# Expert input products of a decoder layer: three 256-column products a weight tile instead of one of 512 and one of 256 columns

## Chip, cores, metric

The kernel runs on one core of a Trainium2 chip. The metric is the device time of one execution in microseconds (us); the median of several runs is compared. TensorE is called PE in the profile (its weight loads PEld), VectorE DVE, ScalarE ACT, GpSimd POOL and SyncE SP.

## What is computed

The reference is one decoder layer on 256 tokens with 2048 channels, in f32: attention and a convolution side by side, then a channel mixer that picks 16 experts for each of 8 heads out of 16384. The change touches the first product of that mixer. Cut to it:

```python
a = jnp.einsum('td,ted->te', x_c, u_emb[e_c])      # x_c: normed tokens, u_emb: 16384 x 2048
coef = (jax.nn.gelu(a) * g_c).astype(v_emb.dtype)
return jnp.einsum('te,ted->td', coef, v_emb[e_c])
```

The kernel doesn't gather. It computes the product of all 16384 experts with all 256 tokens, applies gelu, multiplies by a matrix of gates that is zero where an expert wasn't picked, and multiplies the result by all rows of `peer_v`.

## The kernel before

**The stream.** All large weights go through one stream, whose order is a list made ahead. A piece is 128 x 512 of weights, so four weight tiles of 128 x 128. SP loads two pieces at a time into `raw` (4 buffers). ACT rounds a piece to a short float format, `hi` (L153, 5 buffers), and DVE subtracts it from the full value, `lo` (L159, 4 buffers). Products of PE are then made as hi times hi, hi times lo and lo times hi, which together are near f32. `Stream.piece` issues for piece number p, in this order: the cast `hi` of piece p + 4, the subtraction `lo` of piece p + 3, the matmuls of piece p, and then one step of each job that is under way. A job is a generator that issues a few instructions at each step (evacuations of PSUM, the choice of experts, the scatter of gates), so the place of every instruction in its engine's queue follows from the count of pieces.

**Projections.** `Stream.proj` makes one output tile of 128 x 256 from 16 weight tiles, so 4 pieces. For each weight tile it issues three matmuls of 256 columns into one sum: hi of the weight with hi of the input (L200), hi with lo (L201), lo with hi (L202). `Stream.proj2` makes the same sum in another order: for the four weight tiles of a piece first hi of the weight with 512 columns, which are hi and lo of the input side by side (L213), so that two partial sums lie side by side in a PSUM bank, and then for the four weight tiles lo of the weight with 256 columns of hi, into the second of these sums (L217). Each matmul has a weight load of its own, in both.

**The expert inputs.** 128 tiles `u_tile(i1)` of 4 pieces each, 512 pieces, from 1005.9 us to 1751.2 us of the profiled execution. The input `h2` holds hi and lo of each 128 channels side by side, and `h2hi`, `h2lo` are views of it. The last 8 query projections before it (L1184) use `proj` on these two views; in between stand the score matmuls of a head (L1077, 8 matmuls of 128 columns each). After each tile a job evacuates PSUM: a copy of the second sum to `ut` (ACT L1194 for the first 48 tiles, DVE L1196 for the other 80), an addition of the first sum (DVE L1198), gelu into `C` (ACT L1202), and for tokens whose gates are in `C` already, gelu into `ut` (L1204) and a product (DVE L1208). PSUM has two `acc` buffers.

**Beside it.** During the first 48 tiles DVE works on the choice of experts (`top_steps`), and PE does nothing else, but for the last 8 matmuls of L1077 at the start and three pairs of transposes at the end (L1139). During the other 80 tiles `g_steps` makes the matrix of gates, four tokens at a time: DVE and ACT build one-hot tiles (L1219, L1225), PE multiplies them (L1246, groups of 8 f16 matmuls), and DVE and ACT bring the result into `C` (L1234, L1236). There are 64 such groups, one every four to five pieces. Then follows the output product with `peer_v` (L1333 to L1335, matmuls of 512 columns).

Of the kernel before, what the change touches and what calls it, by code (L numbers as in the profile page):

```python
# [9 lines left out]
F32 = mybir.dt.float32  # L10
# [3 lines left out]
AF = mybir.ActivationFunctionType  # L14
# [5 lines left out]
T = 256  # L20
D = 2048
KT = 16
# [50 lines left out]
def build(nc, tc, d):  # L73
    ctx = ExitStack()
    ve, sc, pe, sp = nc.vector, nc.scalar, nc.tensor, nc.sync
# [53 lines left out]
    class Stream:  # L129
# [63 lines left out]
        def proj(self, bank, nk, xhi, xlo, evac):  # L193

            ps = bank()
            for k0 in range(0, nk, 4):
                def mm(hi, lo):
                    for j in range(4):
                        k, o = k0 + j, j * 128
                        pe.matmul(ps, hi[:, o:o + 128], xhi[:, k], start=(k == 0), stop=False)  # L200
                        pe.matmul(ps, hi[:, o:o + 128], xlo[:, k], start=False, stop=False)  # L201
                        pe.matmul(ps, lo[:, o:o + 128], xhi[:, k], start=False, stop=(k == nk - 1))  # L202
                self.piece(mm)
            return self.add(evac(ps))

        def proj2(self, bank, nk, x, evac):

            ps = bank()
            for k0 in range(0, nk, 4):
                def mm(hi, lo):  # L210
                    for j in range(4):
                        k, o = k0 + j, j * 128
                        pe.matmul(ps.rearrange("p a t -> p (a t)"), hi[:, o:o + 128],  # L213
                                  x[:, k].rearrange("p a t -> p (a t)"), start=(k == 0), stop=False)
                    for j in range(4):
                        k, o = k0 + j, j * 128
                        pe.matmul(ps[:, 1], lo[:, o:o + 128], x[:, k, 0], start=False, stop=(k == nk - 1))  # L217
                self.piece(mm)
            return self.add(evac(ps))

# [33 lines left out]
    S = Stream(plan)  # L254
# [37 lines left out]
    def bank_st(shape):  # L292
        return ps_st.tile(shape, F32, name="ps_st", tag="st", bufs=1)

    ps = bank_st([128, T])
# [175 lines left out]
    def gen_bank(shape, tag="t", bufs=2):  # L471
        return ps_mix.tile(shape, F32, name="ps_" + tag, tag=tag, bufs=bufs)
# [470 lines left out]
    gg = P("gg", side="right")  # L943
    h2p = P("h2p", side="right")
    h2 = h2p.tile([128, KT, 2, T], F32R, name="h2")
    h2hi, h2lo = h2[:, :, 0], h2[:, :, 1]
# [95 lines left out]
    HALF = 48  # L1042
# [143 lines left out]
    tokens, ready = [0], [0]  # L1186

    def u_tile(i1):
        def f(ps):
            n = tokens[0]  # L1190
            cs = C[0][:, i1] if i1 < HALF else C[1][:, i1 - HALF]
            t = gg.tile([128, T], F32, name="ut", tag="ut", bufs=1)
            if i1 < HALF:
                sc.copy(t, ps[:, 1])  # L1194
            else:
                ve.tensor_copy(t, ps[:, 1])  # L1196
            yield
            ve.tensor_add(t, t, ps[:, 0])  # L1198
            yield
            n = tokens[0]  # L1200
            if n < T:
                sc.activation(cs[:, n:], t[:, n:], AF.Gelu_apprx_tanh)  # L1202
            if n > 0:
                sc.activation(t[:, 0:n], t[:, 0:n], AF.Gelu_apprx_tanh)  # L1204
            ready[0] = i1 + 1
            yield
            if n > 0:
                ve.tensor_mul(cs[:, 0:n], cs[:, 0:n], t[:, 0:n])  # L1208
            yield
        return S.proj2(lambda: gen_bank([128, 2, T], "acc"), KT, h2, f)  # L1210

    def g_steps():

# [57 lines left out]
    for i1 in range(HALF):  # L1271
        u_tile(i1)
# [16 lines left out]
    for i1 in range(HALF, NK):  # L1289
        end = u_tile(i1)  # L1290
# [164 lines left out]
```

## Time and profile before

| what | value |
|---|---|
| median of 3 runs | 2459.44 us (2457.65 to 2459.54) |
| the profiled execution | 2461.47 us, span of its instructions 2459.7 us |
| PE busy | 2428.0 us, 99% of the span |
| PEld busy | 2155.9 us, 88% |
| DVE busy | 1938.2 us, 79% |
| ACT busy | 1434.6 us, 58% |
| mean granted clock of TensorE | 0.996 |

A time in a row is in us from the start of the span, a duration in us or ns as the view says. Matmuls overlap in the profile, each lasts longer than the distance to the next, so what a matmul costs is read from the distance between starts, not from its duration. The granted clock is a share of 2.4 GHz; 1.00 is that level and 0.50 would be 1.2 GHz.

### The profile page before, as it was taken

What the parts mean: (1) busy time and instruction counts of PE and PEld (TensorE: products, weight loads), DVE (VectorE), ACT (ScalarE), POOL (GpSimd) and SP (SyncE); (2) the same over time, 40 slices, a digit from 0 to 9 for tenths busy, and PEclk for the clock granted to TensorE, in tenths of its full rate; (3) what the DMA queues carried; (4) which work ended last, traced back from release to release, by engine and by line L of the source; (5) the groups of instructions that cost most, each with busy time, mean ns of one, the idle gap of its engine ahead of it and who ended that gap; (6) DMA issues with size and microseconds to landing.
All of it is one profiled execution on the core that took longest, in us unless ns stands there. A gap on an engine that the chain in (4) does not pass through costs nothing.

```text
span 2459.7 us, 44248 instructions
## 1 busy us (share of the span) xinstructions
PE 2428.0 (99%) x15324; PEld 2155.9 (88%) x15324; DVE 1938.2 (79%) x4120; ACT 1434.6 (58%) x3214; POOL 140.3 (6%) x262
## 2 busy tenths in 40 slices
PE   7999999999999999999999999999999999999999
PEld 6889999988899999988888888888888888888887
DVE  7979896989788877899988888888655566666666
ACT  2145457677455566555568888887555555555554
POOL 0000000211222210000000000000000000100100
PEclk9999999999999999999999999999999999999999
DMA  9965555756888985555555555555565667777765
GB/s 384 402 206 189 182 193 186 248 180 181 300 303 304 324 276 172 181 190 187 192 189 176 175 177 178 175 179 173 188 192 192 191 210 243 242 240 243 242 205 195
DMA packets 155171, 540.50 MB, mean 220 GB/s; under 512 B 18753, under 2 KB 19009, under 8 KB 154689
## 3 DMA queue, kind: packets, MB, share of 16 engines
q1 hardware_dynamic: 134178, 467.40, 56.4%
q0 software_dynamic: 20768, 70.27, 9.3%
q8 instruction: 120, 1.97, 0.3%
q14 instruction: 105, 0.86, 0.1%
HBM read 533.41 MB, written 4.19 MB: 219 GB/s over the span
## 4 chain that ended last, share of the span: by engine, by line
PE 91%; DMA 5%; DVE 3%; issue 1%; ACT 0%; POOL 0%; SPq 0%; POOLq 0%; DVEq 0%; ACTq 0%
PE ps_acc L213 19%; PE ps_acc L217 10%; PE acc L200 8%; PE acc L202 8%; PE acc L201 8%; DMA wa<-in_w_ada_dram 3%; PE ps_o L1333 2%; PE ps_t L1333 2%; PE ps_s L1333 2%; PE ps_o L1335 2%; PE ps_s L1335 2%; PE ps_t L1335 2%; PE ps_acc L1333 2%; PE ps_acc L1335 2%; PE ps_o L1334 2%; PE ps_s L1334 2%
## 5 line engine op out<-in xcount | busy, mean ns | idle before, releaser
L153 ACT CAST hi<-raw 128x512 fp32r<-128x512 f32 x1548 | 955.7, 620 | 810.9 <-PE acc L201 255.5
L159 DVE TENSOR_TENSOR lo<-raw,hi 128x512 fp32r<-128x512 f32 x1548 | 1062.7, 688 | 393.8 <-PE ps_o L1334 77.1
L213 PE MATMUL ps_acc<-h,hi 128*128 128x512 f32 x2048 | 564.6, 397 | 0.0
L213 PEld LDWEIGHTS ps_acc<-h,hi 128*128 128x128 f32 x2048 | 346.8, 188 | 44.1
L217 PEld LDWEIGHTS ps_acc<-h,lo 128*128 128x128 f32 x2048 | 311.5, 188 | 46.4
L200 PE MATMUL acc<-hhi,hi 128*128 128x256 f32 x1200 | 346.7, 289 | 0.0
L202 PE MATMUL acc<-hhi,lo 128*128 128x256 f32 x1200 | 333.9, 278 | 0.2 <-DVE lo L159 0.2
L201 PE MATMUL acc<-hlo,hi 128*128 128x256 f32 x1200 | 333.9, 278 | 0.0
L217 PE MATMUL ps_acc<-h,lo 128*128 128x256 f32 x2048 | 318.0, 277 | 0.0
L200 PEld LDWEIGHTS acc<-hhi,hi 128*128 128x128 f32 x1200 | 226.7, 189 | 6.3 <-issue 5.3
L201 PEld LDWEIGHTS acc<-hlo,hi 128*128 128x128 f32 x1200 | 226.1, 188 | 3.2 <-issue 3.1
L202 PEld LDWEIGHTS acc<-hhi,lo 128*128 128x128 f32 x1200 | 225.4, 188 | 0.4 <-DVE lo L159 0.4
L391 POOL DMA_DIRECT2D adaw<-in_w_ada_dram x192 | 104.7, 546 | 776.4 <-DVE rr L739 277.9
L405 DVE SCALAR_TENSOR_TENSOR ada<-adaw,sc_c,ada 128x512 f32<-128x512 f32 x180 | 134.4, 747 | 13.5 <-DMA adaw<-in_w_ada_dram 13.2
L359 PE MATMUL zb<-hr,w 128*128 128x256 f32 x448 | 107.9, 396 | 11.5 <-ACT hr L339 11.5
L1310 POOL DMA_DIRECT2D g2w<-in_w_ada_dram x64 | 34.3, 537 | 1404.4 <-DVE Alo L123 1098.5
L359 PEld LDWEIGHTS zb<-hr,w 128*128 128x128 f32 x448 | 86.0, 197 | 27.2 <-ACT hr L339 15.8
L1225 ACT ACTIVATE Ahi<-ohA,high 128x128 f16<-128x128 f16 x256 | 100.7, 393 | 10.9 <-PE ps_o L1246 10.7
L491 DVE SCALAR_TENSOR_TENSOR cacc<-glu,dwh,cacc 128x256 f32<-128x256 f32 x240 | 105.1, 475 | 0.0
L1225 ACT ACTIVATE Alo<-ohA,low 128x128 f16<-128x128 f16 x256 | 99.0, 387 | 0.0
L323 DVE SCALAR_TENSOR_TENSOR acc<-wa,sc_c,acc 128x256 f32<-128x256 f32 x224 | 91.8, 479 | 2.1 <-DMA wa<-in_w_ada_dram 2.1
L200 PE MATMUL acc<-ohi,hi 128*128 128x256 f32 x256 | 71.6, 280 | 2.7 <-DVE mr L923 2.7
(371 smaller groups left out, 4525.7 us busy)
## 6 DMA issues: line engine op xcount, KB each, us to landing
raw<-in_u_dram SPq DMA_DIRECT2D x256, 512.0 KB, 3.7
raw<-in_v_dram SPq DMA_DIRECT2D x256, 512.0 KB, 4.5
raw<-in_w_in_dram SPq DMA_DIRECT2D x150, 512.0 KB, 4.3
adaw<-in_w_ada_dram POOLq DMA_DIRECT2D x192, 256.0 KB, 5.1
wa<-in_w_ada_dram SPq DMA_DIRECT2D x64, 512.0 KB, 9.9
raw<-in_nsa_out_dram SPq DMA_DIRECT2D x32, 512.0 KB, 5.5
raw<-in_w_out_dram SPq DMA_DIRECT2D x32, 512.0 KB, 5.7
raw<-in_peer_wq_dram SPq DMA_DIRECT2D x32, 512.0 KB, 4.5
```

Source lines behind the costliest of these rows:

```text
L153: sc.copy(hi, self.source(n))
L159: ve.tensor_sub(lo, self.source(n), hi.bitcast(F32))
L200: pe.matmul(ps, hi[:, o:o + 128], xhi[:, k], start=(k == 0), stop=False)
L201: pe.matmul(ps, hi[:, o:o + 128], xlo[:, k], start=False, stop=False)
L202: pe.matmul(ps, lo[:, o:o + 128], xhi[:, k], start=False, stop=(k == nk - 1))
L213: pe.matmul(ps.rearrange("p a t -> p (a t)"), hi[:, o:o + 128], x[:, k].rearrange("p a t -> p (a t)"), start=(k == 0), stop=False)
L217: pe.matmul(ps[:, 1], lo[:, o:o + 128], x[:, k, 0], start=False, stop=(k == nk - 1))
L359: pe.matmul(zb[n // 2][:, n % 2], ws[k][n // 7][:, n % 7], hr[k], start=(k == 0 and n % 2 == 0), stop=(k == KT - 1), skip_group_check=True)
L405: ve.scalar_tensor_tensor(acc, raw, sc_c[:, k:k + 1], acc, op0=OP.mult, op1=OP.add)
L1225: sc.activation(part[:, j], A[:, j], AF.Copy, scale=g[:, t0 + j:t0 + j + 1])
L1333: pe.matmul(ps, chi, hi, start=(i1 == 0), stop=False)
L1335: pe.matmul(ps, clo, hi, start=False, stop=(i1 == NK - 1))
```

## The change

The expert inputs are made by `proj` on `h2hi` and `h2lo`, as the query projections are, into a PSUM tile of 128 x 256. `proj2` goes. There is one sum, so the copy and the addition go, and gelu reads PSUM; `ut` is only used for tokens whose gates are in `C` already. The evacuation has two steps instead of four. What is streamed, how often, and the number of steps of all other jobs stay.

```diff
-        def proj2(self, bank, nk, x, evac):
-            ps = bank()
-            for k0 in range(0, nk, 4):
-                def mm(hi, lo):
-                    for j in range(4):
-                        k, o = k0 + j, j * 128
-                        pe.matmul(ps.rearrange("p a t -> p (a t)"), hi[:, o:o + 128],
-                                  x[:, k].rearrange("p a t -> p (a t)"), start=(k == 0), stop=False)
-                    for j in range(4):
-                        k, o = k0 + j, j * 128
-                        pe.matmul(ps[:, 1], lo[:, o:o + 128], x[:, k, 0], start=False, stop=(k == nk - 1))
-                self.piece(mm)
-            return self.add(evac(ps))
...
             n = tokens[0]
             cs = C[0][:, i1] if i1 < HALF else C[1][:, i1 - HALF]
-            t = gg.tile([128, T], F32, name="ut", tag="ut", bufs=1)
-            if i1 < HALF:
-                sc.copy(t, ps[:, 1])
-            else:
-                ve.tensor_copy(t, ps[:, 1])
-            yield
-            ve.tensor_add(t, t, ps[:, 0])
-            yield
-            n = tokens[0]
             if n < T:
-                sc.activation(cs[:, n:], t[:, n:], AF.Gelu_apprx_tanh)
+                sc.activation(cs[:, n:], ps[:, n:], AF.Gelu_apprx_tanh)
             if n > 0:
-                sc.activation(t[:, 0:n], t[:, 0:n], AF.Gelu_apprx_tanh)
+                t = gg.tile([128, T], F32, name="ut", tag="ut", bufs=1)
+                sc.activation(t[:, 0:n], ps[:, 0:n], AF.Gelu_apprx_tanh)
             ready[0] = i1 + 1
             yield
             if n > 0:
                 ve.tensor_mul(cs[:, 0:n], cs[:, 0:n], t[:, 0:n])
             yield
-        return S.proj2(lambda: gen_bank([128, 2, T], "acc"), KT, h2, f)
+        return S.proj(lambda: gen_bank([128, T], "acc"), KT, h2hi, h2lo, f)
```

## Rows read from the trace of the kernel before

**Rows 1.** Stretch, length; busy PE, PEld, DVE, ACT, POOL; clock, DMA share, GB/s.
```profile
1074.00:1135.00 61.00, 61.00 (x354) 53.27 (x353) 57.77 (x173) 34.42 (x67) 0.00 (x0) 1.00 0.60 188
1400.00:1500.00 100.00, 100.00 (x649) 87.66 (x648) 81.86 (x174) 82.38 (x229) 0.00 (x0) 1.00 0.53 174
```

**Rows 2.** The same of L213 alone (PE, PEld): unbroken stretch of the first part.
```profile
1012.37:1264.74 252.37, 198.46 (x729) 123.27 (x729) 1.00 0.59 189
```

**Rows 3.** PE in order of time, one piece: start, duration in us.
```profile
1049.81 1.09 PE L213 MATMUL ps_acc<-h,hi 128*128 128x512 f32 x4
1050.73 0.62 PE L217 MATMUL ps_acc<-h,lo 128*128 128x256 f32 x4
1051.19 1.09 PE L213 MATMUL ps_acc<-h,hi 128*128 128x512 f32 x4
```

**Rows 4.** Busy time of L200 alone: the query projections between the score matmuls L1077.
```profile
963.30:972.84 9.54, 7.58 (x27) 4.95 (x27) 1.00 0.52 168
974.09:984.63 10.54, 8.56 (x31) 5.70 (x31) 1.00 0.46 154
985.88:996.83 10.95, 8.71 (x31) 5.70 (x31) 1.00 0.57 184
998.43:1005.91 7.48, 6.07 (x22) 4.02 (x22) 1.00 0.53 165
```

**Rows 5.** The chain that ended last: groups L620 of eight matmuls, projections between.
```profile
370.65 1.01 PE ps_s L620 x8
377.32 1.01 PE ps_s L620 x8
384.19 1.01 PE ps_s L620 x8
```

**Rows 6.** PE in order of time, the last group L1077 and what follows it.
```profile
1008.68 1.05 PE L1077 MATMUL ps_s<-skT,pq 128*128 128x128 f32 x8
1009.49 1.17 PE L213 MATMUL ps_acc<-h,hi 128*128 128x512 f32 x4
1010.50 0.63 PE L217 MATMUL ps_acc<-h,lo 128*128 128x256 f32 x4
1010.97 0.86 PE L213 MATMUL ps_acc<-h,hi 128*128 128x512 f32 x3
```

**Rows 7.** PE in order of time, one group L1246 and what follows it.
```profile
1289.55 0.23 PE L1246 MATMUL ps_o<-Ahi,ohB 128*128 128x128 f16 x1
...
1289.98 1.18 PE L213 MATMUL ps_acc<-h,hi 128*128 128x512 f32 x4
1291.00 0.62 PE L217 MATMUL ps_acc<-h,lo 128*128 128x256 f32 x4
1291.46 0.85 PE L213 MATMUL ps_acc<-h,hi 128*128 128x512 f32 x3
```

**Rows 8.** The same, the first of three pairs of transposes L1139.
```profile
1266.13 0.38 PE L1139 MATMUL ps_t<-cst,I 128*128 128x128 f32 x2
```

**Rows 9.** The tile ut: durations in ns, least, median, most.
```profile
L1198 DVE TENSOR_TENSOR ut<-ut,ps_acc x128: 400/414/418, 1015.2 to 1753.2; 128x256 f32<-128x256 f32 x128
...
L1196 DVE COPY ut<-ps_acc x80: 415/417/422, 1280.2 to 1752.0; 128x256 f32<-128x256 f32 x80
```

**Rows 10.** In order of time: the subtraction that ended latest before its piece, and that piece.
```profile
1254.93 0.69 DVE L159 TENSOR_TENSOR lo<-raw,hi 128x512 fp32r<-128x512 f32 x1
...
1257.81 0.62 PE L213 MATMUL ps_acc<-h,hi 128*128 128x512 f32 x2
```

**Rows 11.** Restart of a projection after L1077: PE in order of time.
```profile
997.64 0.37 PE L200 MATMUL acc<-h,hi 128*128 128x256 f32 x1
...
998.43 0.28 PE L200 MATMUL acc<-h,hi 128*128 128x256 f32 x1
```

**Rows 12.** Busy time of L1333 alone, early and later in the output product.
```profile
1760.00:2010.00 250.00, 143.42 (x364) 68.48 (x365) 1.00 0.60 191
2030.00:2280.00 250.00, 143.08 (x368) 68.94 (x368) 1.00 0.75 243
```

## Prediction

> **What bounds the kernel now.** I read the busy time by stretches first. In both parts of the expert inputs PE is busy for every microsecond, DVE for 57.8 of 61.0 us in the first and 81.9 of 100 us in the second, ACT for 34.4 and 82.4, and the granted clock is 1.00, the 2.4 GHz level [rows 1]. The view of waits then shows no wait of PE in the whole stage. So neither the addition on DVE nor a transfer sets the pace: the stage lasts as long as PE needs to start its matmuls, and only the distance between starts matters.
>
> That distance stands in the rows of L213 alone: 729 records in 252.37 us, one of them cut at the edge, so 728, four a piece and 182 pieces of 1.3867 us [rows 2]. In order of time a piece is 0.92 us for four matmuls of 512 columns and 0.46 us for four of 256 [rows 3]. One of 512 so costs 0.230, one of 256 some 0.115 us: twice as many columns, twice the time. By columns the change is neutral, three times 256 for 512 and 256, and everything hangs on what a 256-column matmul costs when all of them are of that kind.
>
> The kernel shows it already, on the same operands `h2hi` and `h2lo`: the last query projections. Between the groups L1077 they run at a uniform step, and there are two such steps, with nothing in between. 27 weight tiles in 9.54 us and 31 in 10.95 us are 0.3533 us for the three matmuls; 31 in 10.54 us and 22 in 7.48 us are 0.3400 us [rows 4]. The clock is 1.00 in all four rows, so it isn't the clock. I call them the long and the short step. A piece is 12 matmuls: 1.4133 us at the long step, 1.3600 at the short one. The old piece, 1.3867, lies exactly in the middle. The change gains or loses 0.0267 us a piece, by which of the two steps PE falls into.
>
> **Which step.** In the rows a step, once taken, holds until other matmuls come between: each row is unbroken, and the step changes only at the groups L1077, alternating long, short, long, short [rows 4]. The earlier groups L620, also of eight f32 matmuls, do the same: from the first to the second 6.67 us, from the second to the third 6.87 us, with 16 weight tiles in either interval [rows 5]. The difference, 0.20, is 16 times the difference of the steps, 0.21. In the trace all nine groups L620 that come out of the short step lead to the long one. So eight f32 matmuls turn the step over.
>
> **The first part, 187 pieces.** The new kernel enters it at the short step (the last row of [rows 4] runs up to its start, on the same operands). After two pieces the last L1077 comes [rows 6], and by the rule it turns to the long step. The old kernel supports this: the four L217 behind that group take 0.47 us [rows 6], those of an ordinary piece 0.46 [rows 3]. Then PE does nothing else until the first transposes [rows 8]: 185 pieces at +0.0267 are **+4.9 us**, the first two -0.05.
>
> **Eleven pieces around the transposes.** Behind 16 of the 19 pairs of transposes that stand alone between projections (L656, L667) the step is short, whatever it was before: 11 times 0.0267, **-0.3 us**, bound +0.3.
>
> **The second part, 314 pieces.** Each of 64 groups L1246 interrupts it. No projection stands behind such a group in the old trace, so I bound by the two steps, -8.4 and +8.4 us, and choose by the nearest row: behind L1246 the first four L213 take 1.02 us and the L217 0.46 us, against 1.01 and 0.47 behind L1077 [rows 6, 7]. Every one of the 64 groups shows this same form, the one with the short L217. As PE enters a group from 256-column matmuls before and after the change, I take the short step: **-8.4 us**. Restarts are a little dearer: two weight tiles after an interruption take 0.79 us, not 0.68, so 0.11 more [rows 11], where the old piece loses 0.09 (1.02 instead of 0.93) [rows 3, 7]. Some 0.01 to 0.02 us 64 times: **+0.7 us**, bounds 0 and 1.3.
>
> **What goes.** 128 additions of 0.414 us and 80 copies of 0.417 us leave DVE [rows 9], 86 us together, and 48 copies leave ACT. PE waits for none of them, so this is worth nothing, and without the cover of PE it could give at most what DVE is over it, which is below zero in both stretches [rows 1].
>
> **What moves.** gelu comes one to two pieces earlier and reads PSUM; the sum is then done by PE, not by DVE. It is queued behind the hi cast of piece p + 4, which itself waits until PE has read the hi of piece p - 1, two matmuls before that sum ends. So ACT waits about a quarter us at most, with the next hi cast behind it, which has over three pieces of time. PSUM's buffer is free two pieces after its tile, needed four after.
>
> `lo` is read earlier: by the third matmul of a piece, 0.23 us from its start, not 0.92 us [rows 3]. The n-th subtraction belongs to the n-th piece, and pairing all 512, the one that came latest started at 1254.93, took 0.69 and was for the piece at 1257.81 [rows 10]: 2.19 us early. A wait begins only if DVE falls back by another 2.4 us, and it is being relieved. Cost zero; were it to wait, each us late is a us of the whole. `hi` is released some 0.35 us later in its piece, of a lead of over 4 us. No transfer moves.
>
> A rule of the Trainium skill speaks against the change. "TensorE: Matmul & The Clock Gate", section "Wait — 56ns, not 53.3ns?", gives a matmul its columns at 2.4 GHz and a fixed 2.5 ns besides. Three matmuls for two would then be 2.5 ns dearer on each of 2048 weight tiles, an estimate from that page of +5.1 us, 2464.5 in all. The distances here don't follow it: 0.230 us for 512 columns is more than twice the short step's 0.113.
>
> **Sum.** -0.05 + 4.9 - 0.3 - 8.4 + 0.7 = -3.1 us. The profiled execution took 2461.5 us, 1.8 of it around its span, so 2458.4; it lies 2.0 over the median of the runs. On the median, 2459.4, the change gives **2456.3 us**, 0.13% less. Three runs of the old kernel lie 1.9 us apart, so 0.2%, 4.9 us, is about what can be told from no change.
>
> **Rivals.**
> A. Short step in both parts: the last L1077 doesn't turn it. For: why it turns is unknown to me, I have only the pattern. Against: that pattern, without an exception on these operands [rows 4, 5]. 187 times -0.0267 in place of +4.9: 2446.4 us.
> B. Long step in both parts, the other side: L1246 leaves PE at the long step. It decides from some 58 of the 314 pieces at the long step on, where the gain is used up (3.1 / 0.0533). All of them: 2459.4 + 4.9 + 0.3 + 8.4 = 2473.0 us. Against: the form in [rows 7]; for: that form is of 512 columns, not of 256.
> C. L1246 turns the step over each time, as eight f32 matmuls do: the second part is worth nothing, 2459.4 + 4.9 + 0.7 - 0.3 = 2464.7 us. Against: all 64 groups are alike.
> D. A fixed cost for every matmul instead of two steps: 0.1133 us for 256 columns is 6.7 ns over 256 cycles at 2.4 GHz; 2048 more matmuls at that price give +13.7, 2473.1 us. Against: by this the old piece would be 1.333 us long, and it is 1.387 [rows 2].
> E. My sum, and the output product starts at its shorter form. It has two as well: 364 L1333 in 250 us early, 368 later [rows 12], 0.0075 us apart for about 390 of them, the early ones. If the new stage hands over differently, -2.7: 2453.6 us. Against: the last matmuls before it stay 256-column ones.
>
> **Chances.** My sum 0.55, A 0.16, B 0.13, C 0.06, D 0.03, E 0.07. Range: sum, A, C and E hold 0.84, and 2445 to 2465 covers them with a us of spread. Faster by over 0.2% means under 2454.5: A, most of E (0.05), and 0.10 of the sum's 0.55, which lies 1.8 us above that line: 0.31. Slower means over 2464.4: B, D, 0.04 of C: 0.20. The rest, 0.49, is no difference.
>
> **What would show it.** No L213 and no L1196, L1198; DVE busy about 86 us less; the rows of L200 grown by 2048. Unbroken stretches of 0.353 us a weight tile from 1010 to 1266 us, and 0.340 after each L1246; first transposes some 5 us later than before, end of the stage some 3 us earlier. Wrong, if PE waits for `lo`, if steps change inside an unbroken stretch, or if the part behind L1246 is long.

## The result, and the profile after

The changed kernel takes 2477.51 us, the median of four runs (2476.05 to 2478.16); beside them the kernel before took 2458.55 us, also of four (2457.38 to 2459.54). The ratio is 1.0072 with an interval from 1.0057 to 1.0087: slower by 0.7%, some 19 us. Forecast were 2456.3 us and a range to 2465, so it lies above the range, and nearest to the rivals B (2473.0) and D (2473.1).

The page of the changed kernel, its busy times and the groups that the change touches (line, engine, operation, names, shapes, count, then busy us and mean ns):

```profile
span 2474.3 us, 48231 instructions
PE 2442.3 (99%) x17372; PEld 2257.2 (91%) x17372; DVE 1879.5 (76%) x3912; ACT 1413.7 (57%) x3166; POOL 140.3 (6%) x262
...
L200 PE MATMUL ps_acc<-h,hi 128*128 128x256 f32 x2048 | 581.1, 284 | 0.0
L202 PE MATMUL ps_acc<-h,lo 128*128 128x256 f32 x2048 | 575.3, 281 | 0.0
L201 PE MATMUL ps_acc<-h,hi 128*128 128x256 f32 x2048 | 575.3, 281 | 0.0
```

The edit did what it says: L213 and L217 are gone, each of the 2048 weight tiles has three products of 256 columns, and DVE and ACT are relieved. In the two stretches of [rows 1], busy time of all engines (length; PE, PEld, DVE, ACT, POOL; clock, DMA share, GB/s):

```profile
1074.00:1135.00 61.00, 61.00 (x520) 61.00 (x519) 54.29 (x158) 30.10 (x55) 0.00 (x0) 1.00 0.54 186
1400.00:1500.00 100.00, 100.00 (x898) 99.38 (x898) 71.04 (x138) 79.61 (x224) 0.00 (x0) 1.00 0.50 172
```

PE is still busy for all of it, at the same granted clock of 1.00, and the view of waits shows none of PE in the stage. So the loss lies again in the distance between matmuls. The same view of L200 alone (length; PE and PEld busy): three intervals of query projections between the score matmuls, the whole first part of the expert inputs, and two intervals between groups of f16 matmuls (L1246 of before, now L1223):

```profile
970.62:981.18 10.56, 8.56 (x31) 5.72 (x31) 1.00 0.45 151
982.43:993.38 10.95, 8.71 (x31) 5.70 (x31) 1.00 0.55 184
994.63:1005.17 10.54, 8.56 (x31) 5.71 (x31) 1.00 0.50 167
1006.34:1267.53 261.19, 207.67 (x740) 138.69 (x739) 1.00 0.55 186
1291.76:1298.91 7.15, 5.70 (x20) 3.73 (x20) 1.00 0.51 175
1305.51:1312.66 7.15, 5.70 (x20) 3.73 (x20) 1.00 0.48 174
```

The query projections alternate as before (10.54 or 10.56, 10.95, 10.54 for 31 weight tiles; compare [rows 4]). The unbroken first part is 261.19 us for 739 weight tiles, 0.3534 each: the long step, as forecast. Behind the f16 groups 20 weight tiles take 7.15 us: the first takes 0.43 with the restart, and the other 19 have 6.72, 0.354 each. That is the long step too, where I forecast the short one.

The first weight tiles of the first such interval, PE in order of time (start and duration in us). From 1291.76 to 1292.19 it is the restart, from there to 1292.55 one tile of some 0.35:

```profile
1291.73 0.22 PE L1223 MATMUL ps_o<-Alo,ohB 128*128 128x128 f16 x1
1291.76 0.36 PE L200 MATMUL ps_acc<-h,hi 128*128 128x256 f32 x1
...
1292.19 0.28 PE L200 MATMUL ps_acc<-h,hi 128*128 128x256 f32 x1
...
1292.55 0.28 PE L200 MATMUL ps_acc<-h,hi 128*128 128x256 f32 x1
```

**Where the 14.6 us between the two profiled spans are** (2474.3 and 2459.7), from the first matmul of a stage to the first of the next:

| | before | after | difference |
|---|---|---|---|
| ahead of the expert inputs | ends at 1005.91 | ends at 1002.45 | -3.46 |
| first part, to the first transposes | 260.22 | 265.08 | +4.86 |
| 11 pieces around the transposes | 15.96 | 16.21 | +0.25 |
| second part, with its 64 groups | 469.11 | 476.85 | +7.74 |
| output product, first weights (`ohA` to `Alo`) | 269.19 | 274.40 | +5.21 |
| output product, weights `chi`, `clo` | 433.25 | 433.30 | +0.05 |

The first row lies ahead of anything that was changed, and it differs from run to run: in the runs below that leave the tiles where they are, the stage starts between 999.1 (e9) and 1009.4 us (e6). The stages behind it give +18.1, which is the difference of the medians within a us. The fifth row was not in my sum. There the three 512-column matmuls of a weight tile take 0.687 us before and 0.700 after, from start to start, seen in the same view for the first of them (L1333 in [rows 12], now L1310), early and late:

```profile
1764.00:2014.00 250.00, 141.87 (x358) 67.53 (x358) 1.00 0.55 188
2040.00:2290.00 250.00, 142.93 (x368) 69.07 (x368) 1.00 0.72 242
```

358 in 250 us early, where [rows 12] have 364; late 368, as there.

### The profile page after: what moved, and what is told of

Its sections match the earlier page's. It is cut to its first block, busy times and chain, and to the rows that moved or that the text cites. A ratio compares the mean times of both kernels' runs of the same rounds, so it can differ in the third digit from the quotient of the medians.

```text
span 2474.3 us, 48231 instructions
## 1 busy us (share of the span) xinstructions
PE 2442.3 (99%) x17372; PEld 2257.2 (91%) x17372; DVE 1879.5 (76%) x3912; ACT 1413.7 (57%) x3166; POOL 140.3 (6%) x262
## 4 chain that ended last, share of the span: by engine, by line
PE 84%; issue 7%; DVE 3%; DMA 3%; POOL 2%; SPq 0%; ACT 0%; POOLq 0%; DVEq 0%; ACTq 0%
PE ps_acc L200 10%; PE ps_acc L202 10%; PE ps_acc L201 10%; PE acc L200 7%; PE acc L202 7%; PE acc L201 7%; PE ps_o L1312 2%; PE ps_s L1312 2%; PE ps_t L1312 2%; PE ps_o L1311 2%; PE ps_o L1310 2%; PE ps_s L1311 2%; PE ps_t L1310 2%; PE ps_s L1310 2%; PE ps_t L1311 2%
## 5 line engine op out<-in xcount | busy, mean ns | idle before, releaser
L200 PE MATMUL ps_acc<-h,hi 128*128 128x256 f32 x2048 | 581.1, 284 | 0.0
L202 PE MATMUL ps_acc<-h,lo 128*128 128x256 f32 x2048 | 575.3, 281 | 0.0
L201 PE MATMUL ps_acc<-h,hi 128*128 128x256 f32 x2048 | 575.3, 281 | 0.0
L201 PEld LDWEIGHTS ps_acc<-h,hi 128*128 128x128 f32 x2048 | 390.7, 191 | 0.0
L200 PEld LDWEIGHTS ps_acc<-h,hi 128*128 128x128 f32 x2048 | 387.1, 189 | 0.0
L202 PEld LDWEIGHTS ps_acc<-h,lo 128*128 128x128 f32 x2048 | 384.4, 188 | 0.0
L200 PE MATMUL acc<-hhi,hi 128*128 128x256 f32 x1200 | 345.9, 288 | 0.0
L200 PEld LDWEIGHTS acc<-hhi,hi 128*128 128x128 f32 x1200 | 225.9, 188 | 6.3 <-issue 5.3
L344 PEld LDWEIGHTS zb<-hr,w 128*128 128x128 f32 x448 | 86.0, 197 | 26.3 <-ACT hr L324 14.6
```

The costliest lines, as they stand in the source:

```text
L344: pe.matmul(zb[n // 2][:, n % 2], ws[k][n // 7][:, n % 7], hr[k], start=(k == 0 and n % 2 == 0), stop=(k == KT - 1), skip_group_check=True)
```

## The experiments

Each is the changed kernel with the edit shown, unless said otherwise. A time without an interval is one run, and the start of the stage alone moves by some us, so I read the stages in its trace: "stage" is the length of the expert inputs (758.14 us in the changed kernel, 745.30 before), "per tile" the step of the three 256-column matmuls, and "entry form" the three matmuls of 512 columns at the start of the output product (0.700 after, 0.687 before). The expectations name theories by letter (not the rivals A to E of the prediction): **H**, history, how PE resumed after the last interruption decides the step; **P**, where the tiles lie in SBUF decides the step; **L**, a group of eight f16 matmuls always leaves the long step; **K**, such a group keeps the step it was entered with; **W**, the weights of neighbouring matmuls do it; **D**, a short wait for `ohB` at the entry decides the entry form; **S**, the steps of PE's matmuls are the whole of the change.

### Where the tiles lie

Place of the one-hot tiles: `ut` is claimed earlier, as before the change (e1), or the one-hot tiles and h2 move 192 bytes down (e5). Place of h2, of which every projection matmul of the stage streams 256 columns, with the one-hot tiles left in place: down by 192 bytes (e2), 64 (e7), 384 (e8). And the kernel before with h2 down by 192 bytes (e4). The padding tiles are never read. The pools below h2 (`np`, later `ca` with `C`) move with it; no projection matmul of the stage reads them.

```
# e1_ut_first
+            t = gg.tile([128, T], F32, name="ut", tag="ut", bufs=1)
             if n < T:
# e2_h2_pad (e7: 16 words, e8: 96 words; e4: as e2, in the kernel before)
+    h2p.tile([128, 48], F32, name="h2pad")
# e5_gg_pad
-    vp.tile([128, 48], F32, name="tail")
+    gg.tile([128, 48], F32, name="tail")
```

> The changed kernel, but ut is taken first from its pool as in the kernel before, so that the one-hot tiles, which later hold the weights of the output product's first part, lie where they lay before (1024 bytes higher than in the changed kernel). Theory P (place: where the weights and the input of a matmul lie in SBUF, relative to each other, sets the step): the three matmuls of 512 columns of the output product's first part go from 0.700 back to 0.687 us, so the output product is 5.2 us shorter, and the expert inputs stay at 758 us. Theory H (history: the way in which PE comes out of the last interruption sets the step, and the long step of the expert inputs is handed on): the first part stays at 0.700.

> The changed kernel with h2 192 bytes lower in SBUF (an unused tile of 48 words behind it); its distance to the weights is then that which the input and weights of the output product's second part have, where the step was the short one in both kernels. P: every weight tile of the expert inputs takes 0.340 us and not 0.353, the stage some 731 us and not 758 (2048 times 0.0133 us less). H: the same groups of matmuls interrupt in the same order, so 0.353 and 758 us stay.

> The kernel before with h2 192 bytes lower in SBUF, where the 256-column matmuls of the changed kernel took 0.360 us for three and its stage 770.8 us. If the place acts on matmuls of 512 columns too (as in the output product, 0.680, 0.687 or 0.700 for three): a piece other than 1.3867 us, a stage other than 745.3 us. If it acts on the 256-column ones alone, a piece grows by at most a third of what the changed kernel's grew (1.360 or 1.413 to 1.440), so 745 to 759 us.

> The changed kernel with the unused 48 words moved from the pool of the output product's second part to the pool below it, so that h2 as in the run with h2 lowered, and the one-hot tiles too, lie 192 bytes lower, while the second part's weights stay. P: expert inputs at 0.340 us a weight tile (731 us), and the output product's first part at 0.680 us for three matmuls and not 0.700 (7.8 us less over some 390): in all 27 + 8 = 35 us less than the changed kernel, some 2442 us, faster than both. H: no difference from the changed kernel, 2477 us.

> The changed kernel with h2 64 bytes lower in SBUF. 192 bytes lower gave one step alone, 0.360 us a weight tile, whatever came before; at the old place there are two, 0.340 and 0.353. P (the place decides which steps there are): a step other than 0.353, between 0.340 and 0.360, in the query projections on h2 and in the expert inputs alike, so a stage of 731 to 771 us. H alone: 0.353 and 758 us, and the same alternation in the query projections.

> The changed kernel with h2 384 bytes lower, the other side of 192 bytes. P: a step other than 0.353 again; if the distances act symmetrically around that of the run with 192 bytes (0.360), 0.340 or 0.353 as at the old place. H alone: 0.353 and 758 us.

| | one time, us | stage | per tile | entry form |
|---|---|---|---|---|
| changed kernel | 2476.05 | 758.14 | 0.353 | 0.700 |
| e1 | 2476.37 | 758.14 | 0.353 | 0.700 |
| e2 | 2485.89 | 770.81 | 0.360 | 0.687 |
| e7 | 2490.02 | 768.40 | 0.360 and 0.356 | 0.687 |
| e8 | 2472.47 | 758.41 | 0.353 | 0.687 |
| e5 | 2483.62 | 770.81 | 0.360 | 0.680 |
| e4 (before, padded) | 2468.18 | 751.98 | piece of 1.40 | 0.687 |

Busy time of L200 in e2 (length; PE, PEld), inside the first part and inside an interval of the query projections, which stream the same h2:

```profile
973.00:983.00 10.00, 7.77 (x28) 5.18 (x27) 1.00 0.45 151
1009.00:1275.00 266.00, 209.13 (x739) 141.75 (x739) 1.00 0.55 183
```

266.00 us for 739 weight tiles are 0.360. That is a third step, it holds whatever came before (the query projections no longer alternate), and I had expected the short one: P's direction was wrong. But the place does decide which steps there are, since no matmul, no order and no other operand of the projections was changed: 0.340 and 0.353 with h2 where it was; 0.353 alone in e8 and 0.360 alone in e2, in the query projections, in the first part and behind the groups alike; 0.360 in the first part of e7, and behind 41 of its 64 groups 0.356 on the mean, with single weight tiles 0.351 to 0.361 apart. The one-hot tiles' old order gives nothing back (e1), while with both moved the output product enters at 0.680 (e5). Before, the same padding lengthens the piece from 1.387 to 1.40, in order of time:

```profile
1048.84 1.09 PE L213 MATMUL ps_acc<-h,hi 128*128 128x512 f32 x4
1049.77 0.63 PE L217 MATMUL ps_acc<-h,lo 128*128 128x256 f32 x4
1050.24 1.09 PE L213 MATMUL ps_acc<-h,hi 128*128 128x512 f32 x4
```

So the padding costs the old form 6.7 us and the new one 12.7, and at that place the change would cost 18.8 in this stage (770.81 - 751.98). What the change is worth hangs on where h2 happens to lie.

### How the stretch is entered

The last head's score matmuls twice over, 16 instead of 8 (e3); one more transpose behind them, and one more ahead of the output product, both into a bank that nobody reads (e6); the order of the products changed so that neighbouring matmuls load other weight tiles (e9); e6 and one more transpose in each pair of L1139 (e10, timed in three rounds).

```
# e3_twice
-        for tt in range(2):
+        for tt in (0, 1, 0, 1) if h == PH - 1 else range(2):
# e6_one_more
+        if h == PH - 1:
+            pe.transpose(u_bank([128, 128], "t"), ident, ident)
...
+    pe.transpose(u_bank([128, 128], "t"), ident, ident)   # ahead of the output product
# e9_by_product
+                    for w, x in ((hi, xhi), (hi, xlo), (lo, xhi)):
+                        for j in range(4):
# e10_third: e6 and
-            for tt in range(2):
+            for tt in (0, 1, 1):
```

> The changed kernel, where the score matmuls of the last head are issued twice (16 instead of 8, the same result), which costs 0.8 us once. H, as my prediction had it (eight such matmuls turn the step over): the first part of the expert inputs, 185 pieces, goes to the short step, 0.340 us a weight tile, and is 9.9 us shorter, less the 0.8. P alone, without history: it stays at 0.353 us, and the stage is 0.8 us longer.

> The changed kernel with one transposing matmul of 128 columns more at two places, its result unused: behind the last score matmuls L1077 (ahead of the expert inputs) and between the expert inputs and the output product. Place of all operands as in the changed kernel. H (history chooses among the steps that the place allows): at least one of the two stretches behind it changes its step, the first part of the expert inputs from 0.353 to 0.340 us a weight tile (9.9 us less), or the output product's first part from 0.700 to 0.687 us (5.2 us less). If the step doesn't depend on how PE is entered: 0.353 and 0.700, and 0.2 us more.

> The changed kernel with another order within a piece of the expert inputs: hi by hi for its four weight tiles, then hi by lo, then lo by hi, so the same 12 matmuls of 256 columns, each with its weight load, but no two behind each other with the same weights. Theory W (the weights of neighbours, twice the same and then others, make the long step): a uniform step of 0.340 us for three, 731 us for the stage. Theory P and H: the distances in SBUF are of the same kind, so the step stays one of 0.340 and 0.353, and as PE comes in as before, the long one, 758 us.

> The changed kernel with the two single matmuls of the run before (behind the last L1077, and ahead of the output product), and a third transpose in each of the three pairs L1139 (a repetition of the second, same result). In the changed kernel and in the run with one matmul more all 64 groups L1246 were entered at the long step and left at it. Theory K (a group L1246 keeps the step with which it is entered, as it does in the kernel before): entered at the short step, all of the second part stays there, 0.340 us a weight tile, 314 pieces times 0.0533 us = 16.7 us less, the stage some 732 us, and the whole about 2443 us, faster than both kernels. Theory L (an L1246 group always leaves the long step): the second part as before at 476.9 us and the whole about 2467 us.

e3: still 0.353, stage 759.03 with the eight extra matmuls, entry form 0.700, 2478.44 us. "Eight turn it over" would have given the short step after 16; in this form the rule is refuted. e9: stage 758.14 and entry form 0.700, to the hundredth as without it, 2472.62 us: W falls.

e6 took 2468.21 us, and its stage is 748.43. PE in order of time at the start of the first part, and the same stretches of L200 by busy time:

```profile
1012.16 1.05 PE L1062 MATMUL ps_s<-skT,pq 128*128 128x128 f32 x8
1013.05 0.27 PE L1064 MATMUL ps_t<-cst 128*128 128x128 f32 x1
1013.08 0.37 PE L200 MATMUL ps_acc<-h,hi 128*128 128x256 f32 x1
```
```profile
1013.29:1264.78 251.49, 204.13 (x740) 138.73 (x739) 1.00 0.59 193
1289.01:1296.16 7.15, 5.70 (x20) 3.73 (x20) 1.00 0.54 180
```

One matmul of 0.27 us, with no operand of the stage, brings 740 weight tiles from 261.19 to 251.49 us: 0.340 each, the short step. The second part, where nothing was changed, stays at 7.15 us an interval. And the output product's entry form is 0.687 behind its one extra transpose. So history decides, and one matmul is enough.

e10 asks what the f16 group does. Its third transpose brings PE to the first group at the short step (12.01 us for 35 weight tiles and the restart), and behind the group it is long again:

```profile
1265.32:1277.33 12.01, 9.69 (x36) 6.56 (x35) 1.00 0.60 195
...
1285.35:1292.50 7.15, 5.70 (x20) 3.73 (x20) 1.00 0.54 178
```

K falls, L stands with h2 at this place: the group of eight leaves the long step in all 64 intervals (second part 476.88, stage 748.27). Only the first of them was entered at the short one. Timed, e10 is level with the kernel before: 2461.59 against 2460.29, ratio 1.0002 [0.9989, 1.0014].

### A ninth matmul in the group, and the old evacuation

e6, and ahead of each group of eight one f16 matmul whose sum the first of the eight overwrites: of 128 columns (e11, again as e14 in five rounds) or 32 (e15, as e17 in five rounds).

```
# e11_nine, e14_nine_timed: e6 and
+                pe.matmul(ps[:, 0], B[:, 0], parts[0][:, 0], start=True, stop=True)
# e15_ninth_32, e17_ninth_timed: e6 and
+                pe.matmul(ps[:, 0, 0:32], B[:, 0], parts[0][:, 0, 0:32], start=True, stop=True)
```

> The changed kernel with the two single matmuls of the run before and a ninth f16 matmul in each of the 64 groups L1246 (ahead of the others and overwritten by the first of them, same result), 64 times some 0.06 us = 3.6 us more. K: the ninth matmul moves the restart, so the step behind the groups can change: if the short step is hit and kept, 16.7 - 3.6 = 13 us less than the run without it. L: 476.9 + 3.6 us in the second part.

> The run with a ninth f16 matmul in each group and the two single matmuls, repeated for its time: expert inputs 737 us, output product's first part at 0.687 us, so 745.3 - 737.0 = 8.3 us less than the kernel before, ratio some 0.9966. If the choice of steps isn't stable from execution to execution, the ratio lies nearer to 1 and the runs spread by more than 3 us.

> The same with a ninth matmul of 32 columns instead of 128, so cheaper by up to 64 times 0.04 us = 2.6 us. If any matmul more in the group leads to the short step: expert inputs some 734.5 us. If the time by which the restart is moved matters (theory H in its narrow form: PE comes out of the interruption at another moment): the long step may come back, second part 314 pieces times 0.0533 us longer, so 751 us.

> The run with a ninth matmul of 32 columns, repeated for its time: expert inputs 734.0 us against 745.3 of the kernel before, 11.3 us less, output product as before, ratio some 0.9954.

PE of e17 in order of time at a group, and L200's busy time in the first part and behind that group:

```profile
1283.51 0.19 PE L1223 MATMUL ps_o<-Ahi,ohB 128*128 128x32 f16 x1
1283.55 0.22 PE L1226 MATMUL ps_o<-Ahi,ohB 128*128 128x128 f16 x1
...
1283.94 0.22 PE L1226 MATMUL ps_o<-Alo,ohB 128*128 128x128 f16 x1
1283.97 0.36 PE L200 MATMUL ps_acc<-h,hi 128*128 128x256 f32 x1
...
1284.40 0.28 PE L200 MATMUL ps_acc<-h,hi 128*128 128x256 f32 x1
...
1284.74 0.28 PE L200 MATMUL ps_acc<-h,hi 128*128 128x256 f32 x1
```
```profile
1008.46:1259.95 251.49, 204.12 (x740) 138.70 (x739) 1.00 0.58 193
1283.97:1290.87 6.90, 5.61 (x20) 3.73 (x20) 1.00 0.53 177
```

Behind nine matmuls the restart is as dear as behind eight (0.43 us for the first weight tile), and then the tiles are 0.34 apart, 6.90 us an interval where eight gave 7.15. The second part falls from 476.88 (e10) to 465.47 with the ninth of 128 columns, and to 462.48 with that of 32. The stage is 737.02 and 734.03 us.

Both beat the two kernels. e14: 2452.51 against 2459.77 before, ratio 0.9965 [0.9951, 0.9979]. e17: 2448.96 against 2460.02, ratio 0.9950 [0.9933, 0.9967]. It is the best version here, the change with 66 useless matmuls.

Last in this group, the products of the change with the evacuation of before (two sums of 256 columns, copy, addition, gelu from SBUF):

```
# e12_old_evac
+                        pe.matmul(ps[:, 0], hi[:, o:o + 128], xhi[:, k], start=(k == 0), stop=(k == nk - 1), skip_group_check=True)
+                        pe.matmul(ps[:, 1], hi[:, o:o + 128], xlo[:, k], start=False, stop=False, skip_group_check=True)
+                        pe.matmul(ps[:, 1], lo[:, o:o + 128], xhi[:, k], start=False, stop=(k == nk - 1), skip_group_check=True)
...
+            ve.tensor_add(t, t, ps[:, 0])
```

> The changed kernel's matmuls (three of 256 columns for a weight tile, hi by hi into one half of a bank, the other two into the other half) with the evacuation of the kernel before: copy, addition on DVE, gelu from SBUF. Theory S (the steps of PE's matmuls are the whole of the change, the evacuation is worth nothing): expert inputs 758 us, output product's first part at 0.700 us, whole some 2477 us, as the changed kernel. If the shorter evacuation gives or takes time of its own, the stage differs from 758 us.

L200 in its first part, and the first matmul of the output product (now L1331):

```profile
1008.56:1269.75 261.19, 207.67 (x740) 138.69 (x739) 1.00 0.56 186
```
```profile
1790.00:2020.00 230.00, 131.96 (x335) 62.98 (x335) 1.00 0.58 192
```

One time of 2473.03 us, stage 758.14: to the hundredth that of the change. The whole loss of the stage is in the matmuls, and the shorter evacuation is worth nothing in it. But the entry form is 0.687 again: 335 in 230 us, where 0.700 would give 329.

### The entry to the output product

`ohB`, the weight of the third matmul there, is computed at the very end of the expert inputs. DVE gets one useless copy (e13) or two (e16) ahead of it.

```
# e13_late_ohB (e16_later_ohB: the copy twice)
+    w0 = gg.tile([128, T], F32, name="ut", tag="ut", bufs=1)
+    ve.tensor_copy(w0, iota[:, 0:1].to_broadcast([128, T]))
```

> The changed kernel with one useless copy of 128 x 256 on DVE (some 0.3 to 0.4 us, its result unused) ahead of the first subtraction that makes the lo weights ohB of the output product. In the changed kernel that subtraction ended 0.18 us before PE loaded these weights; in the kernel before and in the run with the old evacuation PE had to wait a few hundredths of a us for it, and went on at 0.687 us for three matmuls, not 0.700. Theory D (that short wait is what takes PE out of the longest step): the first part goes to 0.687 us, 5.2 us less than the changed kernel, with the expert inputs unchanged at 758 us. Otherwise 0.700 us.

> The run with one useless copy ahead of the first subtraction for ohB, with two copies. One copy took 0.29 us, but ohB was ready 0.17 us before its load all the same, so PE didn't wait and the run tried nothing. Two copies should make PE wait some 0.1 us. Theory D (a short wait at that place takes PE out of the longest step): output product's first part at 0.687 us for three matmuls, 5.2 us less than the changed kernel. Otherwise it stays at 0.700.

e13 decides nothing: `ohB` was still ready 0.17 us before its load, no wait arose, the form stayed 0.700 (2476.85 us). In e16, in order of time:

```profile
1762.27 0.42 DVE L123 TENSOR_TENSOR ohB<-C,ohA 128x256 fp32r<-128x256 f32 x1
...
1762.52 0.39 PE L1314 MATMUL ps_o<-lo,ohA 128*128 128x512 f32 x1
...
1762.74 0.19 PEld L1315 LDWEIGHTS ps_o<-hi,ohB 128*128 128x128 f32 x1 [0.26 <-DVE ohB L123]
1762.75 0.49 PE L1315 MATMUL ps_o<-hi,ohB 128*128 128x512 f32 x1
```
```profile
1790.00:2020.00 230.00, 131.29 (x336) 62.87 (x335) 1.00 0.59 192
```

The weight load waits, 0.26 us by the view, and the next 390 or so weight tiles go at 0.687 (the second view is of their first matmul, L1313): the first part of the output product is 269.29, not 274.40 us, and the run takes 2472.62. D stands as far as this: a short wait at the entry is enough to leave the 0.700 form. It isn't needed: e2, e7 and e8, with h2 elsewhere, and e6, with a transpose more, enter at 0.687 without one.

The same entry in the kernel before, and in the changed one:

```profile
1751.02 0.42 DVE L123 TENSOR_TENSOR ohB<-C,ohA 128x256 fp32r<-128x256 f32 x1
...
1751.43 0.40 PE L1334 MATMUL ps_o<-lo,ohA 128*128 128x512 f32 x1
1751.49 0.19 PEld L1335 LDWEIGHTS ps_o<-hi,ohB 128*128 128x128 f32 x1
```
```profile
1760.22 0.43 DVE L123 TENSOR_TENSOR ohB<-C,ohA 128x256 fp32r<-128x256 f32 x1
...
1760.83 0.40 PE L1311 MATMUL ps_o<-lo,ohA 128*128 128x512 f32 x1
1760.83 0.19 PEld L1312 LDWEIGHTS ps_o<-hi,ohB 128*128 128x128 f32 x1
```

Before, the product for `ohB` ends at 1751.44 and its load starts at 1751.49, 0.06 us behind the matmul ahead of it: a wait too short for the view to name. After, `ohB` is done at 1760.65 and the load starts together with that matmul, at 1760.83. e12, which brings the copy and addition back to DVE, again has `ohB` late (its load 0.03 us behind) and again 0.687. With h2 at its place and no transpose more, the form goes with this in every run: 0.687 where the load comes late (before, e12, e16), 0.700 where it starts with that matmul (changed kernel, e1, e3, e9, e13). So the likeliest cause of the 5.2 us is that the relieved DVE is on time. That a wait has this effect is shown by e16; that these 0.03 to 0.06 us are the cause in the two kernels is argued from the rows.

## Why the prediction was wrong

**What held.** PE bounds the stage, by the distance of its matmuls and not by the clock or a wait; both were seen again. The work taken from DVE and ACT is worth nothing in the stage (e12). `lo` and gelu cause no wait of PE. DVE's busy time fell by 58.7 us (1938.2 before), not by the 86 of the removed rows; what the rest of it is I did not follow, since DVE sets no pace here. There is nothing between the two steps on these operands at their place. First part: +4.9 forecast, +4.86 measured, and the first two pieces at the short step, as forecast. Restarts: I priced 64 of them at +0.7; the second part came out at +7.74, where 314 pieces at the long step give +8.4, so they are about -0.6. The 11 pieces around the transposes are +0.25, at the bound of +0.3, not at -0.3.

**The step that failed** is the choice for the second part: "Every one of the 64 groups shows this same form, the one with the short L217. As PE enters a group from 256-column matmuls before and after the change, I take the short step: -8.4 us." Measured is the long step behind every group, rival B: -8.4 became +8.4, some 17 us of the 21 by which I was off. The form was a difference of 0.01 us in the first four matmuls behind a group, of 512 columns, and of 0.01 us the other way in the four of 256 columns behind them; the old stage has only one distance, 1.387 a piece, behind L1077 and behind L1246 alike. It could not tell which step 256-column matmuls would take there, and I had said so under B ("that form is of 512 columns, not of 256") and given B too little weight for it. By the rows, both bounds were equally near. Rival D's 2473.1 is as near to the result as B's by luck: it wants one cost for every 256-column matmul, and the same 739 weight tiles take 261.19 us in the changed kernel and 251.49 in e6.

**The rule beneath it**, that eight f32 matmuls turn the step over, gave the right step for the first part, and so +4.9, in the sequence as it stood, and is not a rule: 16 do not turn it back (e3), and a ninth, of another kind, does (e6). What the runs show is that the step of a whole stretch is chosen where PE resumes, by the exact sequence there, and that where the streamed tile lies sets which steps there are.

**The term that was missing.** I assumed the output product's form unchanged because "the last matmuls before it stay 256-column ones", and my rival E let it only become shorter. It became longer, +5.2 us, most likely for want of a wait of 0.06 us. Without it the stage's +12.84 alone, on the median of before, would have been 2471.4 us, near B's 2473.0.

**What stays open** is why. Runs with h2 at four places and with eight, nine or sixteen matmuls ahead show that place and resumption both matter; none shows what in SBUF or in PE's reads makes 0.340, 0.353 or 0.360 of the same three matmuls, nor which place would be best.

The rule of the Trainium skill that I weighed ("TensorE: Matmul & The Clock Gate", section "Wait — 56ns, not 53.3ns?": its columns at 2.4 GHz and a fixed 2.5 ns for each matmul) would have given 109.2 ns for 256 columns, an estimate from that page. No run here shows it: the three steps are 113.3, 117.8 and 120.0 ns a matmul. Its sign was right, but by that cost the step could not differ between e6 and the changed kernel, as it does.

## What to carry to other kernels

When PE bounds a stage by back-to-back matmuls, compare two forms by the measured distance on the same operands, look for more than one such distance, and where the rows show two, forecast both signs instead of picking one from a hundredth of a us in rows of another shape. Then try the cheap perturbations: one useless matmul ahead of a stretch, a tile moved by some hundred bytes. Here 66 such matmuls moved the time of the changed kernel by some -1.2% (e17) and a moved tile by up to +0.5% (e7, one run), around an edit that was itself worth +0.7%. And a wait that a change takes away may have been setting the pace of what follows, so a stage behind the edit has to be compared too.

## What the runs showed of the hardware that I had not expected

- Three f32 matmuls of 256 columns, each with its weight load, have at least three steady distances at a granted clock of 1.00: 0.340, 0.353 and 0.360 us. Three of 512 have 0.680, 0.687 and 0.700.
- A distance, once taken, held for 740 weight tiles, 251 or 261 us, without a break. One matmul of 0.27 us ahead of it changed which (e6), and eight or nine f16 matmuls, one of them of only 32 columns, gave 7.15 or 6.90 us for the next 20 weight tiles (e10, e17).
- Moving the streamed tile by 192 bytes took the stage from 758.14 to 770.81 us, by 384 bytes to 758.41 (e2, e8).
- A wait of PE can pay: 0.26 us of it made the next 269 us 5.1 us shorter (e16).
